# Gate sums per head, and the out-projection's adds at a higher priority, in a hybrid decoder trunk

## The chip, the cores and the metric

The kernel runs on one core of a Trainium2 chip. A core has five engines that run at the same time, each through its own list of instructions in order: TensorE (PE, matmuls), VectorE (DVE), ScalarE (ACT), GpSimd (POOL) and SyncE (SP, which issues DMAs). They wait for each other by semaphores. The metric is the device time of one execution in microseconds, the median of several.

## The reference, cut to what matters

Two residual layers over 512 tokens of width 1024, each followed by a SwiGLU network. The first layer joins a state-space group (16 heads) and a gated linear attention group (GLA, 4 heads), and projects both out. The second is latent attention. The change lies in the first layer, in the GLA group and in the output projection.

```python
def gla_mixer(q, k, v, g, gk_low, gk_w2, gk_b, norm_w):
    gk = jax.nn.log_sigmoid((gk_low @ gk_w2 + gk_b).astype(jnp.float32)) / GLA_GATE_NORM
    gcum = jnp.cumsum(gk.reshape(bsz, nc, Q, H, DK), axis=2)     # within chunks of 64 tokens
    g_last = gcum[:, :, -1]
    q_dec = q * jnp.exp(gcum)
    k_inv = k * jnp.exp(-gcum)
    k_end = k * jnp.exp(g_last[:, :, None] - gcum)
    scores = jnp.where(causal, jnp.einsum('bcihd,bcjhd->bchij', q_dec, k_inv), 0)
    ...
    o = rms_norm(o, norm_w) * jax.nn.silu(g.reshape(bsz, seqlen, H, DV))

def ssd_gla_layer(h, w_in, ..., w_out):
    ...
    return jnp.concatenate([y_ssd, y_gla], axis=-1) @ w_out

x = x + ssd_gla_layer(rms_norm(x, mix_norm_even), ...)
x = x + swiglu(rms_norm(x, ffn_norm[0]), ...)
x = x + mla_layer(rms_norm(x, mix_norm_odd), ...)
x = x + swiglu(rms_norm(x, ffn_norm[1]), ...)
```

## The kernel before

Features lie on the 128 partitions and the 512 tokens along the free dimension. The residual is eight tiles `X[0]` to `X[7]` of 128 x 512 (named x0 to x7), which stay in the on-chip memory. Each product is made of 128 x 512 outputs in one of three PSUM banks (`acc`, line 66), taken in rotation: the next product can only write a bank once the reader of the product three before is done with it.

Every weight arrives by DMA as float32 (`wraw`, two buffers), is split on chip into a rounded part `whi` (ScalarE, line 154) and a rest `wlo` (VectorE, line 155, three buffers each), and each product of a weight block with a split activation is three matmuls (`mm3`, lines 160 to 162). `dense` runs `mm3` over its activation blocks: 24 matmuls for 8 blocks, 12 for 4.

The order on each engine is not written out by hand. A list scheduler orders the instructions by priority, which falls with the place in the program; `tc.high_priority(offset=n)` moves what stands in it ahead by n places. Weights are issued with an offset of 90 (`AHEAD`). Once scheduled, each engine runs its list strictly in order.

The out-projection has four rounds (`out_round`, line 296), each over four of the 16 blocks of 128 mixed features. A round makes eight products of 12 matmuls, numbered 0 to 7 here, two for each weight, and adds product m to `X[m]` (line 304). That add is also what frees the product's `acc` bank. Round 0 runs in the state-space group's last step (line 539), round 1 behind the first GLA head's products (line 706), round 2 and round 3 near the end of the GLA group (lines 717 and 719). In round 3 each finished `X[m]` is also split, squared and summed for the next norm (`Norm.add`).

The GLA group starts with the gates of all heads (lines 571 to 583): a small product per head, ScalarE's Abs, Exp and Ln over the tile `ga` (128 x 2048, four heads side by side), VectorE's minimum into the tile `gm`; then one subtraction over the 2048 columns (line 580) and four running sums, one per head (line 582). `project(h)` makes head h's q and k products and scales them with exponentials of the running sum (tiles e1, e2, e3, el; qd, qp, ki, ke, kp). `inner(h)` makes the scores (lines 644 to 648) in the single bank `a1`, copies them under the mask (lines 651 and 652), transposes kp into the same bank (line 658), and goes on with the state products.

Of the kernel before, what the change touches and what calls it, by code (L numbers as in the profile page):

```python
# [13 lines left out]
ALU = mybir.AluOpType  # L14
# [9 lines left out]
KH = HID // P  # L24
EPS = 1e-6
AHEAD = 90
FIRST = 400
STEPS = 150
VALUES = (2, 3, 7)
# [19 lines left out]
def kernel(ctx: ExitStack, tc: tile.TileContext, A, yT, stop=99):  # L49
    nc = tc.nc  # L50
    V, S, G, E = nc.vector, nc.scalar, nc.gpsimd, nc.tensor
# [9 lines left out]
    def nm(s):  # L61
        cnt[0] += 1
        return f"{s}_{cnt[0]}"

    def acc():
        return pacc.tile([P, T], F32, tag="acc", name=nm("acc"))
# [11 lines left out]
    def aux(tag="st"):  # L78
        while isinstance(phase["tags"][tag], str):
            tag = phase["tags"][tag]  # L80
        return phase["p"].tile([P, T], F32, tag=tag, name=nm(tag), bufs=phase["tags"][tag])
# [4 lines left out]
    X = []  # L86
# [14 lines left out]
    ps = acc()  # L101
# [38 lines left out]
    def weight(src, kc, m):  # L140

        with tc.high_priority(offset=AHEAD):
            return weight_now(src, kc, m)

    def weight_now(src, kc, m):
        raw = wp.tile([P, KD * P], F32, tag="wraw", name=nm("wraw"), bufs=2)
        r = raw[:, :kc * m]
        nc.sync.dma_start(r.rearrange("p (k m) -> p k m", k=kc), src)
        return parts(r, kc, m)
# [14 lines left out]
    def dense(ps, w, xs):  # L164

        n = len(xs)
        for k, (xh, xl) in enumerate(xs):
            last = mm3(ps, w[0][:, k, :], w[1][:, k, :], xh, xl, k == 0, k == n - 1)
        return last
# [40 lines left out]
    def rstd_log(ssq, n, pool, tag):  # L210

        hi = const.tile([P, T], F32R, tag="rsa", name=nm("rsa"))
        lo = const.tile([P, T], F32R, tag="rsb", name=nm("rsb"))
        S.copy(hi, ssq)
        V.tensor_tensor(lo, ssq, hi.bitcast(F32), ALU.subtract)
        ps = aux()
        E.matmul(ps, ones_r, hi, start=True, stop=False)
        E.matmul(ps, ones_r, lo, start=False, stop=True)
        R = pool.tile([P, T], F32, tag=tag, name=nm(tag), bufs=1)
        S.activation(R, ps, AF.Ln, scale=1.0 / n, bias=eps)  # L220
        S.activation(R, R, AF.Exp, scale=-0.5)
        m, t = ssq, const.tile([P, T], F32, tag="rsa", name=nm("rst"))
        V.tensor_scalar(m, ps, 1.0 / n, EPS, ALU.mult, ALU.add)
        V.tensor_tensor(t, R, R, ALU.mult)
        V.scalar_tensor_tensor(t, m, -0.5, t, ALU.mult, ALU.mult)
        V.scalar_tensor_tensor(R, t, 1.5, R, ALU.add, ALU.mult)
        return R
# [61 lines left out]
    with tc.tile_pool(name="sq0", bufs=4) as sq0:  # L289
        for c in range(KD):  # L290
            nrm.square(c, nrm.last, sq0, 4)
        with tc.high_priority(offset=FIRST):
            R = rstd_log(nrm.ssq, D, res, "R")
    xp = nrm.parts

    def out_round(r, parts, nxt=None):

        for m2 in range(4):
            w = weight(A["w_out"][r, m2], 4, 256)
            for j in range(2):  # L300
                m = 2 * m2 + j
                ps = acc()
                dense(ps, (w[0][:, :, j * P:(j + 1) * P], w[1][:, :, j * P:(j + 1) * P]), parts)
                V.tensor_tensor(X[m], X[m], ps, ALU.add)
                if nxt is not None:
                    nxt.add(m)

# [7 lines left out]
    with tc.tile_pool(name="gkp", bufs=1) as gkp:  # L315

        ps = aux("a1")
# [60 lines left out]
        with tc.tile_pool(name="ssd", bufs=2) as sp:  # L378
# [144 lines left out]
            for f in range(8):  # L523
                g = f // 4
                if f % 4 == 0:
                    bc = group(g)
                    if f:
                        bc = spread(*bc)
                    ys, ssq = [], None
                xs = nxt_xs if f == 1 else conv(f, "xs", 3)  # L530
                if f == 0:
                    with tc.high_priority(offset=STEPS):
                        dt, act, acd = steps(mm[0])
                zg = z_gate(f)
                if f == 0:
                    nxt_xs = conv(1, "xs", 3)
                    bc = spread(*bc, mm[1])
                if f == R0F:
                    out_round(0, rounds[0])
                if f == VALUES[0]:  # L540
                    rtok = tok_scalar(R)
                if f in VALUES:
                    values(VALUES.index(f))
                y = core(f, xs, zg, *bc)
                ys.append(y)
                sq = res.tile([P, T], F32, tag="sq", name=nm("ysq"), bufs=2)
                S.activation(sq, y, AF.Square)
                if ssq is not None:
                    V.tensor_tensor(sq, ssq, sq, ALU.add)
                ssq = sq  # L550
                if f % 4 == 3:
                    rounds.append(group_norm(g, ys, ssq))
# [3 lines left out]
        with tc.tile_pool(name="gla", bufs=2) as gp:  # L556
            rmask = gp.tile([P, T], F32, name="rmask", bufs=1)
# [13 lines left out]
            ga = gp.tile([P, 4, T], F32, name="ga", bufs=1)  # L571
            gm = gp.tile([P, 4, T], F32, name="gm", bufs=1)
            for h in range(4):
                ps = aux()
# [2 lines left out]
                V.tensor_scalar(gm[:, h, :], ps, col("gk_b", h), 0.0, ALU.add, ALU.min)  # L577
            S.activation(ga, ga, AF.Exp, scale=-1.0)
            S.activation(ga, ga, AF.Ln, bias=1.0)
            V.tensor_tensor(gm, gm, ga, ALU.subtract)  # L580
            for h in range(4):
                V.tensor_tensor_scan(gm[:, h, :], rmask, gm[:, h, :], 0.0, ALU.mult, ALU.add)
            gcum = gm

            scb = []
# [4 lines left out]
            def project(h):  # L590

                gc = gcum[:, h, :]
                gc8 = gc.rearrange("p (c j) -> p c j", c=8)

                el = gp.tile([P, 8], F32, tag="el", name=nm("el"))
                S.activation(el, gc8[:, :, 63], AF.Exp, scale=1.0 / 16)
                el2 = el.rearrange("p (r two) -> p r two", two=2)

                w = weight(A["w_q"][h], KD, P)
                ps = acc()  # L600
                dense(ps, w, xp)
                e1 = gp.tile([P, T], F32, tag="e1", name=nm("e1"))
                S.activation(e1, gc, AF.Exp, scale=1.0 / 16)
                qd = gp.tile([P, T], F32, tag="qd", name=nm("qd"))
                V.scalar_tensor_tensor(qd, ps, P ** -0.5, R, ALU.mult, ALU.mult)
                V.tensor_tensor(qd, qd, e1, ALU.mult)

                qp = gp.tile([P, 4, 2, 64], F32, tag="qp", name=nm("qp"))
                qd4 = qd.rearrange("p (r two j) -> p r two j", r=4, two=2)
                S.copy(qp[:, :, 0, :], qd4[:, :, 0, :])  # L610
                V.tensor_tensor(qp[:, :, 1, :], qd4[:, :, 1, :],
                                el2[:, :, 0:1].to_broadcast([P, 4, 64]), ALU.mult)

                w = weight(A["w_k"][h], KD, P)
                ps = acc()
                last = dense(ps, w, xp)
                kr = gp.tile([P, T], F32, tag="kr", name=nm("kr"))
                V.tensor_tensor(kr, ps, R, ALU.mult)
                e2 = gp.tile([P, T], F32, tag="e1", name=nm("e1"))
                S.activation(e2, gc, AF.Exp, scale=-1.0 / 16)  # L620
                ki = gp.tile([P, T], F32, tag="ki", name=nm("ki"))
                V.tensor_tensor(ki, kr, e2, ALU.mult)
                e3 = gp.tile([P, T], F32, tag="e1", name=nm("e3"))
                V.tensor_tensor(e3.rearrange("p (c j) -> p c j", c=8),
                                gc8[:, :, 63:64].to_broadcast([P, 8, 64]), gc8, ALU.subtract)
                S.activation(e3, e3, AF.Exp, scale=1.0 / 16)  # L626
                ke = kr
                V.tensor_tensor(ke, kr, e3, ALU.mult)
                kp = gp.tile([P, 4, 2, 64], F32, tag="kp", name=nm("kp"))
                ke4 = ke.rearrange("p (r two j) -> p r two j", r=4, two=2)  # L630
                V.tensor_tensor(kp[:, :, 0, :], ke4[:, :, 0, :],
                                el2[:, :, 1:2].to_broadcast([P, 4, 64]), ALU.mult)
                S.copy(kp[:, :, 1, :], ke4[:, :, 1, :])

                return (qd, qp, ki, ke, kp, el2), last
# [58 lines left out]
            def outer(h, os):  # L694
# [8 lines left out]
                return parts  # L703

            q0, _ = project(0)
            out_round(1, rounds[1])
            q1, last = project(1)
            o0 = inner(0, *q0, last)
            q2, last = project(2)
            o1 = inner(1, *q1, last)  # L710
            p01 = outer(0, o0)
# [58 lines left out]
    with tc.tile_pool(name="mla", bufs=2) as mp, tc.tile_pool(name="mla1", bufs=1) as m1:  # L770
# [30 lines left out]
        ps = acc()  # L801
# [10 lines left out]
        for who, n0, n in (("q", 0, 3), ("kv", 3, 2)):  # L812
            lora[who], ssq = [], None
            for c in range(n):
                w = weight(A["w_dqkv"][n0 + c], KD, P)
                ps = acc()
# [12 lines left out]
            ps = aux()  # L829
# [22 lines left out]
        ps = aux()  # L852
# [14 lines left out]
        ps = aux()  # L867
# [247 lines left out]
```

## Time and profile before

| | us |
|---|---|
| median of 3 runs (1372.68 to 1377.39) | 1374.68 |
| the profiled execution | 1372.01 |
| its span, first to last instruction | 1369.8 |
| PE busy in the span | 1344.3 |
| VectorE busy | 811.9 |
| ScalarE busy | 567.8 |
| mean granted TensorE clock | 0.999 |

A profile is one execution. The span is what its views are measured against; 2.2 us lie around it. In a timeline row stand the start, the time taken, the engine, the line of the kernel, the operation, the tiles (output, arrow, inputs), the shape, and in brackets how long the engine had been idle before and what ended that. Two operations of VectorE overlap by a little, so their starts are closer than their durations.

### The profile page before, as it was taken

To read this page: it belongs to the slowest core of one execution; us is meant where nothing else is said; L and a number is where in the kernel's file an instruction comes from. 1 tells how busy PE (TensorE), PEld (TensorE's weight loads), DVE (VectorE), ACT (ScalarE), POOL (GpSimd) and SP (SyncE) were. 2 spreads that over 40 slices of the span, in tenths; PEclk is the share of its full clock that TensorE was granted. 3 is DMA by queue.
4 is the path that set the end of the run, shared out by engine and by line. 5 is a ranking of instruction groups with operands and counts; after the bars stand their busy time and mean duration, and the time that the engine had idled before them with its cause. 6 is when DMAs were issued, how large, how long until landed. Compare 5 with 4: busy or idle time off the path is not lost.

```text
span 1369.8 us, 16681 instructions
## 1 busy us (share of the span) xinstructions
PE 1344.3 (98%) x6506; PEld 1088.3 (79%) x6506; DVE 811.9 (59%) x1364; ACT 567.8 (41%) x946; POOL 7.8 (1%) x35
## 2 busy tenths in 40 slices
PE   9999999899999999999999999999999999999998
PEld 5798789678888888888888887667588888888887
DVE  7887976778967444444333469776594444443221
ACT  7575623544344322332232348775652322322121
POOL 0000000000000000000000000000000000000000
PEclk9999999999999999999999999999999999999999
DMA  5342232312223233333333321111033333323331
GB/s 177 109 153 79 77 100 73 93 51 89 62 92 106 94 93 105 96 92 95 94 100 100 101 63 59 42 47 62 1 95 105 93 93 101 99 93 108 111 104 63
DMA packets 36781, 122.22 MB, mean 89 GB/s; under 512 B 4768, under 2 KB 5792, under 8 KB 36704
## 3 DMA queue, kind: packets, MB, share of 16 engines
q1 hardware_dynamic: 35888, 120.72, 28.6%
q8 instruction: 51, 0.84, 0.3%
q10 hardware_dynamic: 816, 0.46, 0.1%
q14 instruction: 26, 0.21, 0.1%
HBM read 119.03 MB, written 2.13 MB: 88 GB/s over the span
## 4 chain that ended last, share of the span: by engine, by line
PE 88%; DVE 7%; ACT 3%; issue 1%; DMA 1%; SPq 0%; DVEq 0%; ACTq 0%
PE acc L160 26%; PE acc L161 26%; PE acc L162 26%; PE sco L968 2%; PE ptr L982 1%; PE po L991 1%; DVE wlo L155 1%; PE a L485 1%; PE a L677 1%; DVE cva L397 1%; ACT whi L154 0%; PE a L666 0%; DMA acb<-acd 0%; PE a L471 0%; PE a L679 0%
## 5 line engine op out<-in xcount | busy, mean ns | idle before, releaser
L160 PE MATMUL acc<-xh,whi 128*128 128x512 f32 x1144 | 449.6, 393 | 7.4 <-ACT e L626 4.7
L154 ACT CAST whi<-wraw 128x1024 fp32r<-128x1024 f32 (+2 forms) x221 | 225.8, 1022 | 550.2 <-PE acc L161 449.5
L162 PE MATMUL acc<-xh,wlo 128*128 128x512 f32 x1144 | 448.7, 392 | 0.0
L161 PE MATMUL acc<-xl,whi 128*128 128x512 f32 x1144 | 448.1, 392 | 0.0
L155 DVE TENSOR_TENSOR wlo<-wraw,whi 128x1024 fp32r<-128x1024 f32 (+2 forms) x221 | 261.8, 1185 | 159.3 <-ACT whi L154 159.1
L160 PEld LDWEIGHTS acc<-xh,whi 128*128 128x128 f32 x1144 | 215.2, 188 | 53.2 <-ACT e L626 5.0
L162 PEld LDWEIGHTS acc<-xh,wlo 128*128 128x128 f32 x1144 | 215.1, 188 | 45.1 <-issue 0.7
L161 PEld LDWEIGHTS acc<-xl,whi 128*128 128x128 f32 x1144 | 215.3, 188 | 44.4 <-issue 1.0
L162 PE MATMUL acc<-fhh,wlo 128*128 128x512 f32 x288 | 112.0, 389 | 0.0
L160 PE MATMUL acc<-fhh,whi 128*128 128x512 f32 x288 | 112.0, 389 | 0.0
L161 PE MATMUL acc<-fhl,whi 128*128 128x512 f32 x288 | 112.0, 389 | 0.0
L740 DVE TENSOR_TENSOR fu<-acc,R 128x512 f32<-128x512 f32 x44 | 30.4, 691 | 136.8 <-PE acc L162 136.8
L737 DVE TENSOR_TENSOR fg<-acc,R 128x512 f32<-128x512 f32 x44 | 30.4, 691 | 89.4 <-PE acc L162 89.3
L161 PEld LDWEIGHTS acc<-fhl,whi 128*128 128x128 f32 x288 | 54.1, 188 | 11.3
L162 PEld LDWEIGHTS acc<-fhh,wlo 128*128 128x128 f32 x288 | 54.1, 188 | 11.2
L160 PEld LDWEIGHTS acc<-fhh,whi 128*128 128x128 f32 x288 | 54.1, 188 | 11.1
L161 PE MATMUL acc<-mxl,whi 128*128 128x512 f32 x128 | 50.0, 392 | 0.0
L160 PE MATMUL acc<-mxh,whi 128*128 128x512 f32 x128 | 49.7, 391 | 0.0
L162 PE MATMUL acc<-mxh,wlo 128*128 128x512 f32 x128 | 49.7, 390 | 0.0
L968 PE MATMUL sco<-kT,qT 96*128 96x128 f32 (+3 forms) x128 | 42.8, 445 | 1.5 <-DVE mx L971 1.3
L971 DVE CUSTOM_DVE_ANT_0 sc<-sco,am 128x128 f32<-128x128 f32 (+3 forms) x64 | 30.7, 487 | 13.6 <-PE sco L968 11.5
L973 ACT ACTIVATE sc<-sc,mx 128x128 f32<-128x128 f32 (+3 forms) x64 | 35.7, 561 | 7.3 <-DVE mx L971 7.0
(345 smaller groups left out, 1583.8 us busy)
## 6 DMA issues: line engine op xcount, KB each, us to landing
wraw<-in_w_gate_dram SPq DMA_DIRECT2D x44, 512.0 KB, 3.5
wraw<-in_w_up_dram SPq DMA_DIRECT2D x44, 512.0 KB, 3.5
wraw<-in_w_down_dram SPq DMA_DIRECT2D x32, 512.0 KB, 3.6
wraw<-in_w_out_dram SPq DMA_DIRECT2D x16, 512.0 KB, 3.6
wraw<-in_w_xbc_dram SPq DMA_DIRECT2D x12, 512.0 KB, 3.7
wraw<-in_w_down_dram SPq DMA_DIRECT2D x16, 384.0 KB, 3.1
wraw<-in_w_z_dram SPq DMA_DIRECT2D x8, 512.0 KB, 3.6
wraw<-in_w_v_dram SPq DMA_DIRECT2D x8, 512.0 KB, 3.5
```

The lines of the kernel that those rows point to most:

```text
L154: S.copy(hi[:, :kc * m], r)
L155: V.tensor_tensor(lo[:, :kc * m], r, hi.bitcast(F32)[:, :kc * m], ALU.subtract)
L160: E.matmul(out, ah, bh, start=first, stop=False)
L161: E.matmul(out, ah, bl, start=False, stop=False)
L162: return E.matmul(out, al, bh, start=False, stop=last)
L397: V.scalar_tensor_tensor(a, xpad[:, k:k + T], cw[:, 12 * k + i:12 * k + i + 1], a, ALU.mult, ALU.add)
L485: E.matmul(pd[64 * h:64 * h + 64, c * P:(c + 1) * P], xdt[:, c, h, :], mt[:, h, c, :], start=True, stop=True)
L737: V.tensor_tensor(g, pg, R, ALU.mult)
L740: V.tensor_tensor(u, pu, R, ALU.mult)
L968: E.matmul(ps[:, :n], qts[j][:, b * P:(b + 1) * P], kts[j][:, :n], start=True, stop=True)
L971: V.tensor_tensor_reduce(sc[:, :n], ps[:, :n], am[:, T - n:], -scale, 3e38, ALU.add, ALU.min, mx[:, j:j + 1])
L973: S.activation(sc[:, :n], sc[:, :n], AF.Exp, bias=mx[:, j:j + 1], scale=-1.0, accum_out=sm[:, j:j + 1])
```

## The change

The subtraction over all four heads and the four running sums are taken out of the gates' part. In their place each head's `project(h)` begins with that head's subtraction and running sum. And each add of an out-projection round is issued with a priority offset of 150 places.

```diff
 AHEAD = 90
+FREE = 150
...
                 dense(ps, (w[0][:, :, j * P:(j + 1) * P], w[1][:, :, j * P:(j + 1) * P]), parts)
-                V.tensor_tensor(X[m], X[m], ps, ALU.add)
+                with tc.high_priority(offset=FREE):
+                    V.tensor_tensor(X[m], X[m], ps, ALU.add)
                 if nxt is not None:
...
             S.activation(ga, ga, AF.Ln, bias=1.0)
-            V.tensor_tensor(gm, gm, ga, ALU.subtract)
-            for h in range(4):
-                V.tensor_tensor_scan(gm[:, h, :], rmask, gm[:, h, :], 0.0, ALU.mult, ALU.add)
             gcum = gm
...
                 gc = gcum[:, h, :]
+                V.tensor_tensor(gc, gc, ga[:, h, :], ALU.subtract)
+                V.tensor_tensor_scan(gc, rmask, gc, 0.0, ALU.mult, ALU.add)
                 gc8 = gc.rearrange("p (c j) -> p c j", c=8)
```

The scheduler's lists show what moved. PE's and SP's lists keep their order but for one place (below). The names carry buffer numbers here: x5 is `X[5]`, and most lines of the changed kernel stand one or two further down (the add is L304 before and L306 after; the subtraction moves from L580 to L592, the running sum from L582 to L593).

VectorE from add 4 of round 1 on, before:

```order
L304 TENSOR_TENSOR x4_79<-x4_79,acc_432_2522 128x512
L580 TENSOR_TENSOR gm_2335<-gm_2335,ga_2334 128x2048
L155 TENSOR_TENSOR wlo_449_2628<-wraw_447_2625,whi_448_2627 128x1024
L582 SCALAR_TENSOR_TENSOR gm_2335<-rmask_2320,gm_2335 128x512 x4
L606 TENSOR_TENSOR qd_408_2398<-qd_408_2398,e1_407_2396 128x512
L622 TENSOR_TENSOR ki_416_2439<-kr_414_2435,e1_415_2437 128x512
L611 TENSOR_TENSOR qp_409_2401<-qd_408_2398,el_402_2363 128x4x64
L624 TENSOR_TENSOR e3_417_2441<-gm_2335 128x512
L304 TENSOR_TENSOR x5_81<-x5_81,acc_433_2536 128x512
L304 TENSOR_TENSOR x6_83<-x6_83,acc_437_2556 128x512
L628 TENSOR_TENSOR kr_414_2435<-kr_414_2435,e3_417_2441 128x512
L304 TENSOR_TENSOR x7_85<-x7_85,acc_438_2570 128x512
```

The same place of VectorE's list, now:

```order
L306 TENSOR_TENSOR x4_79<-x4_79,acc_432_2519 128x512
L592 TENSOR_TENSOR gm_2335<-gm_2335,ga_2334 128x512 x2
L306 TENSOR_TENSOR x5_81<-x5_81,acc_433_2533 128x512
L593 SCALAR_TENSOR_TENSOR gm_2335<-rmask_2320,gm_2335 128x512
L156 TENSOR_TENSOR wlo_449_2627<-wraw_447_2624,whi_448_2626 128x1024
L306 TENSOR_TENSOR x6_83<-x6_83,acc_437_2553 128x512
L607 TENSOR_TENSOR qd_408_2395<-qd_408_2395,e1_407_2393 128x512
L623 TENSOR_TENSOR ki_416_2436<-kr_414_2432,e1_415_2434 128x512
L612 TENSOR_TENSOR qp_409_2398<-qd_408_2395,el_402_2360 128x4x64
L625 TENSOR_TENSOR e3_417_2438<-gm_2335 128x512
L306 TENSOR_TENSOR x7_85<-x7_85,acc_438_2567 128x512
L593 SCALAR_TENSOR_TENSOR gm_2335<-rmask_2320,gm_2335 128x512
```

Two subtractions of 512 columns and one running sum now stand where one subtraction of 2048 columns and four running sums stood, and adds 5 and 6 stand ahead of head 0's scalings.

Further on in VectorE's list, at the start of head 1's scalings (qd of buffer 445), before:

```order
L662 TENSOR_TENSOR ed_459_2690<-el_402_2363 128x4
L662 TENSOR_TENSOR ed_495_2854<-el_439_2584 128x4
L605 SCALAR_TENSOR_TENSOR qd_445_2619<-acc_443_2592,R_32_192 128x512
L606 TENSOR_TENSOR qd_445_2619<-qd_445_2619,e1_444_2617 128x512
L155 TENSOR_TENSOR wlo_485_2792<-wraw_483_2789,whi_484_2791 128x1024
```

And now:

```order
L663 TENSOR_TENSOR ed_459_2689<-el_402_2360 128x4
L592 TENSOR_TENSOR gm_2335<-gm_2335,ga_2334 128x512
L663 TENSOR_TENSOR ed_495_2855<-el_439_2583 128x4
L592 TENSOR_TENSOR gm_2335<-gm_2335,ga_2334 128x512
L593 SCALAR_TENSOR_TENSOR gm_2335<-rmask_2320,gm_2335 128x512
L606 SCALAR_TENSOR_TENSOR qd_445_2618<-acc_443_2591,R_32_192 128x512
L593 SCALAR_TENSOR_TENSOR gm_2335<-rmask_2320,gm_2335 128x512
L607 TENSOR_TENSOR qd_445_2618<-qd_445_2618,e1_444_2616 128x512
L156 TENSOR_TENSOR wlo_485_2793<-wraw_483_2790,whi_484_2792 128x1024
```

The subtractions and running sums of heads 2 and 3 have come in between. The scores' copies of head 0 follow some rows later in both.

The one place where PE's list changes is the start of the first SwiGLU network, where the two matmuls of the norm's sum (rsa and rsb) stand among the first product's last matmuls. Before:

```order
L160 MATMUL acc_3853<-xh_3790,whi_3849 128x512
L161 MATMUL acc_3853<-xl_3791,whi_3849 128x512
L162 MATMUL acc_3853<-xh_3790,wlo_3850 128x512
L160 MATMUL acc_3853<-xh_3811,whi_3849 128x512
L161 MATMUL acc_3853<-xl_3812,whi_3849 128x512
L192 MATMUL st_3829<-rsa_3825,ones_r 128x512
```

And now:

```order
L161 MATMUL acc_3856<-xh_3793,whi_3852 128x512
L193 MATMUL st_3832<-rsa_3828,ones_r 128x512
L162 MATMUL acc_3856<-xl_3794,whi_3852 128x512
L163 MATMUL acc_3856<-xh_3793,wlo_3853 128x512
L194 MATMUL st_3832<-rsb_3829,ones_r 128x512
L161 MATMUL acc_3856<-xh_3814,whi_3852 128x512
```

Both matmuls of the sum come four places earlier.

## The prediction

> **What bounds the kernel now.** I read the page first: busy times, then the chain that ended last.
>
> ```profile
> PE 1344.3 (98%) x6506; PEld 1088.3 (79%) x6506; DVE 811.9 (59%) x1364; ACT 567.8 (41%) x946; POOL 7.8 (1%) x35
> ...
> PE 88%; DVE 7%; ACT 3%; issue 1%; DMA 1%; SPq 0%; DVEq 0%; ACTq 0%
> ```
>
> PE (TensorE) is busy for 1344.3 of 1369.8 us, and nothing in the change removes a matmul. So the change can only be worth what it does to PE's idle time, 25.5 us, and to the rate at which PE runs. The view of waits, for PE alone, tells where the largest piece lies; the window around it tells the rate.
>
> ```profile
> PE acc L160 <- ACT e L626: 4.7, 1, 4.7
> PE acc L160 <- ACT qT L951: 3.0, 2, 1.6
> ```
> ```profile
> 262.10 0.39 PE L162 MATMUL acc<-mxh,wlo 128*128 128x512 f32 x1
> 267.15 0.47 PE L160 MATMUL acc<-xh,whi 128*128 128x512 f32 x1 [4.66 <-ACT e L626]
> 267.70 0.63 PE L162 MATMUL acc<-xh,wlo 128*128 128x512 f32 x1
> ...
> 271.34 0.39 PE L162 MATMUL acc<-xh,wlo 128*128 128x512 f32 x1
> ...
> 279.50 0.39 PE L162 MATMUL acc<-xh,wlo 128*128 128x512 f32 x1
> ```
> ```profile
> 267.00:271.00 4.00, 3.85 (x10) 3.14 (x11) 3.42 (x8) 1.23 (x4) 0.00 (x0) 0.58 0.00 0
> ...
> 780.00:1000.00 220.00, 209.26 (x1071) 153.42 (x1070) 161.83 (x456) 144.26 (x326) 1.75 (x3) 1.00 0.16 51
> ```
>
> One wait alone, 4.66 us, is the longest of the whole execution. It falls between out-projection round 1 (its last matmul is at 262.10) and head 1's q product (first matmul at 267.15). Behind it the matmuls take 0.63 us, and in that window the granted clock is 0.58 (the third column from the end); from 271.34 they take 0.39 again.
>
> What ends the wait? The view names the exponential of L626, but this product does not read it. It needs a free bank of `acc` (three banks in rotation), its weights, and xh/xl. VectorE's timeline shows the bank:
>
> ```profile
> 254.37 0.69 DVE L304 TENSOR_TENSOR x<-x,acc 128x512 f32<-128x512 f32 x1
> 256.38 2.29 DVE L580 TENSOR_TENSOR gm<-gm,ga 128x2048 f32<-128x2048 f32 x1 [1.32 <-ACT ga L579]
> 258.59 1.22 DVE L155 TENSOR_TENSOR wlo<-wraw,whi 128x1024 fp32r<-128x1024 f32 x1
> 259.72 4.56 DVE L582 TENSOR_TENSOR_SCAN gm<-rmask,gm 128x512 f32<-128x512 f32 x4
> 264.21 0.66 DVE L606 TENSOR_TENSOR qd<-qd,e 128x512 f32<-128x512 f32 x1
> 264.79 0.68 DVE L622 TENSOR_TENSOR ki<-kr,e 128x512 f32<-128x512 f32 x1
> 265.39 0.41 DVE L611 TENSOR_TENSOR qp<-qd,el 128x256 f32<-128x256 f32 x1
> 265.73 0.68 DVE L624 TENSOR_TENSOR e<-gm 128x512 f32<-128x512 f32 x1
> 266.33 1.27 DVE L304 TENSOR_TENSOR x<-x,acc 128x512 f32<-128x512 f32 x2
> 267.52 0.68 DVE L628 TENSOR_TENSOR kr<-kr,e 128x512 f32<-128x512 f32 x1
> 268.13 0.67 DVE L304 TENSOR_TENSOR x<-x,acc 128x512 f32<-128x512 f32 x1
> ```
>
> Matmuls follow each other by 0.227 us (271.34 to 279.50 holds 36), so a product of 12 takes 2.72. Counting back from 262.10, products 5, 6 and 7 of the round are finished at 257.05, 259.77 and 262.49. Their adds run at 266.33 (two) and 268.13, behind the gates' subtraction, four scans and head 0's scalings. The first add ends at about 267.0, and PE starts at 267.15. The bank is the cause; L626 merely ended at about the same time.
>
> **The change, step by step.** The work in VectorE's queue is a little more than before; its order is what changes. I walk the new order with the durations above: 0.60 us from one 512-wide operation to the next, 0.34 for the 256-wide one, 1.13 for a scan or a weight split (258.59 to 259.72). ScalarE bounds it:
>
> ```profile
> 254.43 1.92 ACT L579 ACTIVATE ga<-ga 128x2048 f32<-128x2048 f32 x1
> 256.86 1.06 ACT L154 CAST whi<-wraw 128x1024 fp32r<-128x1024 f32 x1 [0.52 <-PE acc L161]
> 260.97 0.22 ACT L596 ACTIVATE el<-gm 128x8 f32<-128x8 f32 x1 [1.75 <-DVE gm L582]
> 262.30 1.04 ACT L154 CAST whi<-wraw 128x1024 fp32r<-128x1024 f32 x1
> ```
>
> Subtractions of heads 0 and 1 at 256.38 and 256.98; add 5 at 257.58; scan 0 at 258.18; head 1's k split at 259.31 (its cast ended at 257.92); add 6 at 260.44 (product done 259.77); head 0's qd, ki, qp, e3 at 261.04, 261.64, 262.24, 262.58 (el and the exponentials follow scan 0 from 259.4); add 7 at 263.18. Head 1's q product finds its bank free at 258.3, its k product at 261.1, and the weights of both are split by 260.5. So PE goes on at 262.10 + 0.23 = 262.33 in place of 267.15: **4.82 us**. With the pause goes the slow stretch behind it: 267.15 to 279.50 is 12.35 us for 47 steps, and 47 x 0.2267 is 10.65, so **1.70 us**. Together 6.52.
>
> What is late next? Scans and subtractions of heads 2 and 3 now stand among head 1's scalings, ahead of head 0's masked score copies (L651, L652). These free the one bank `a1`, in which PE's transposes of kp (L658) come next.
>
> ```profile
> 281.26 0.73 DVE L651 COPY_PREDICATED sc<-tri_i,a 64x512 f32<-64x512 int32 x1
> 281.88 0.67 DVE L628 TENSOR_TENSOR kr<-kr,e 128x512 f32<-128x512 f32 x1
> 282.58 0.46 DVE L652 COPY_PREDICATED sc<-tri_i,a 64x256 f32<-64x256 int32 x1
> ```
> ```profile
> 283.30 0.49 PE L658 MATMUL a<-ident,kp 128*128 128x128 f32 x3
> ```
>
> Before, L652 ended at 283.04 and L658 ran at 283.30 with no wait: 0.26 us to spare. Going on: scan 1 at 263.78, head 0's ke 264.91, q split of head 2 at 265.51, kp, ed, two subtractions, then scan 2 at 268.35, head 1's qd 269.48, scan 3 at 270.08, the product with e1 271.2, k split 271.8, qp 272.9, e3 273.3, kr 273.9, ki 274.6, L651 275.2, ke 275.8, L652 at 276.5 until 276.96. PE comes to L658 at 283.30 - 6.52 = 276.78. A wait of about **0.2 us**. Its bounds: nothing, and all four added pieces late, 2 x 0.69 + 2 x 1.2 = 3.8 us. I take 0.2, since the walk uses rows of the same instructions.
>
> A rule speaks against splitting the subtraction. One 2048-wide row takes 2.29 us; the neighbouring 512-wide rows take 0.66 to 0.69. The Trainium skill, "VectorE: DVE Perf Modes", section on the TRN2 errata, says that a fixed latency is paid per instruction, so one large tile pays it once and four pay it four times. This trace agrees in direction: 4 x 0.69 is 2.76 against 2.29. By that rule 0.47 us of queue is added; were all of it on PE's path, the sum below would be 5.8 in place of 6.3. The walk gives the four pieces the time of 512-wide rows, and only two of them stand ahead of an add.
>
> The other rounds. Round 0 and the end of round 3 have these rows:
>
> ```profile
> 185.74 1.23 DVE L155 TENSOR_TENSOR wlo<-wraw,whi 128x1024 fp32r<-128x1024 f32 x1 [0.56 <-ACT whi L154]
> 195.76 0.69 DVE L304 TENSOR_TENSOR x<-x,acc 128x512 f32<-128x512 f32 x1 [2.03 <-PE acc L162]
> ```
> ```profile
> 417.45 0.69 DVE L304 TENSOR_TENSOR x<-x,acc 128x512 f32<-128x512 f32 x1 [0.49 <-PE acc L162]
> ...
> 421.12 0.68 DVE L257 TENSOR_TENSOR sq<-sq,sq 128x512 f32<-128x512 f32 x1
> ```
> ```profile
> 421.84 0.62 ACT L189 CAST rsa<-sq 128x512 fp32r<-128x512 f32 x1 [1.51 <-DVE sq L257]
> ```
> ```profile
> 422.51 0.50 PE L192 MATMUL st<-rsa,ones_r 128*128 128x512 f32 x1
> ```
>
> In round 0 the split of 185.74 comes behind one more add, a convolution tap and a sum, at about 188.2. It is for products 6 and 7, and product 6 starts when product 5 is done, at 195.7: six us of cover. I cost it at nothing; without cover it would be the 2.4 us of its delay. In round 3 the norm's matmul L192 stands four matmuls earlier on PE, 422.51 - 0.9 = 421.6 on the old clock. What it waits for moves too: block 6's split and sum (some 1.25 us) now go ahead of add 7, which runs at about 417.7 in place of 417.45, so the last sum starts at about 420.1 in place of 421.12, and the cast ends near 421.5. That is a tie; I take nothing, between a wait of 0.9 if the sum were no earlier and no gain, since PE did not wait there. SP's weight DMAs keep their order and are issued as splits free the raw buffers; the k split of 258.59 moves to 259.31, 0.7 us later, against a load that is needed two products later.
>
> Sum: 6.52 - 0.2 = **6.3 us**. The profiled execution took 1372.01 us (span 1369.8 and 2.2 around it), so 1365.7 for its like. That execution lies 2.67 below the median shown, 1374.68; the same gain from the median gives **1368.4 us**.
>
> **Rivals.**
> 1. The pause goes, the slow clock was not always there. A pause of 4.66 us need not lower the clock in each execution; one profile shows one. Then the gain is 4.82 - 0.2 = 4.6, and the time 1370.1. For it: from 780 to 1000 PE idles for 10.7 us in pieces of up to 1.6, and the granted clock is 1.00 there, so somewhere between 1.6 and 4.7 us lies what a pause may last. Against it: in this trace it did happen, at 0.58. The Trainium skill, "TensorE: Matmul & The Clock Gate", section "What's actually happening", says that the half rate follows a whole idle window of about 3.4 us which runs freely, so that its phase decides; the trace agrees that a pause of 4.66 us can do it, and no row here shows the phase.
> 2. The stall moves to L658. All of 3.8 us arrives there: 6.5 - 3.8 = 2.7, time 1372.0. For it: the spare time was only 0.26 us, and PE is now 6.5 us earlier. Against: the walk.
> 3. No effect. If L626 were the true releaser, or the adds stayed behind the scans: 1374.7. Against: the order lists add 5 ahead of all scans, and the product does not read L626's tile.
> 4. Slower. VectorE runs in order, so an add put ahead blocks what is behind it until its product ends (the row at 195.76 shows 2.03 us of it). If a weight split stands behind it and the very next product needs that split, PE waits 0.69 + 1.22 = 1.9 us per pair of products. Four rounds have 16 pairs; at half of them 15 us are lost, and the time is 1374.7 - 6.3 + 15 = 1383. It decides from four pairs on. Against it: round 0's split has six us of cover.
>
> **How the numbers follow.** Forecast 60%, rival 1 20%, rival 2 8%, no effect 6%, slower 6%. The three runs of before lie 2.0 below to 2.7 above their median; I give the forecast 1366 to 1371 for that, a us more below, since the profiled execution was already under the lowest run, and reach to rivals 1 and 2 above: 1365 to 1373. That leaves out rivals 3 and 4 and the tails. A measurement of this kernel can tell about 0.3%, 4.1 us, from no change, so faster means below 1370.6. The forecast gives that 92 times in 100, rival 1 60, rival 2 15: 0.55 + 0.12 + 0.01 = 0.68. Slower 0.06 and a tail, 0.07. The rest, 0.25, is within.
>
> **What would show it.** In the changed profile: no PE wait over 0.5 us between the round's last matmul and head 1's q product; every matmul there at 0.39 us; add 5 at about 257.6 ahead of the first scan; head 0's kp transposes with a wait of 0 to 0.5 us on VectorE; the span near 1363.5. I am wrong if a PE wait of several us shows at L658, or at the weights of a round, or if the pause remains under another name.

## The result, and the profile after

| | before | changed |
|---|---|---|
| median of 6 runs, us | 1373.22 | 1365.81 |
| lowest to highest | 1371.39 to 1377.39 | 1365.41 to 1367.81 |
| the profiled execution | 1372.01 | 1365.41 |
| its span | 1369.8 | 1363.2 |

The ratio of the medians is 0.9946, with a 95% interval of 0.993 to 0.9962. The changed kernel is faster by 7.4 us, 0.4 to 0.7%. The forecast was 1368.4 us with a gain of 6.3.

The page of the changed kernel's profile, its span, its busy times and its chain by engine:

```profile
span 1363.2 us, 16686 instructions
...
PE 1342.8 (99%) x6506; PEld 1088.0 (80%) x6506; DVE 812.1 (60%) x1367; ACT 567.9 (42%) x946; POOL 7.8 (1%) x35
...
PE 89%; DVE 7%; ACT 2%; issue 1%; DMA 1%; SPq 0%; DVEq 0%; ACTq 0%
```

The work is the same but for three more instructions on VectorE (1367 for 1364, 0.2 us more). What PE has lost is idle time: 1363.2 - 1342.8 is 20.4 us, for 25.5 before. Its busy time is 1.5 us shorter at the same 6506 matmuls, so some of them run at a higher rate.

Its view of waits for PE (in total, times, longest), over the whole execution first and then for 255 to 300 us alone:

```profile
PE acc L161 <- ACT qT L952: 2.9, 2, 1.6
...
PE a L659 <- DVE sc L653: 0.2, 1, 0.2
```

The longest wait is now one of the attention stage that was there before. Of the wait of 4.7 us nothing is left, and the transposes of kp have a new one of 0.2. PE's timeline around the place (start, time taken) shows both:

```profile
261.41 0.39 PE L163 MATMUL acc<-mxh,wlo 128*128 128x512 f32 x1
261.64 0.39 PE L161 MATMUL acc<-xh,whi 128*128 128x512 f32 x1
...
272.29 0.39 PE L163 MATMUL acc<-xh,wlo 128*128 128x512 f32 x1
276.45 0.52 PE L659 MATMUL a<-ident,kp 128*128 128x128 f32 x3 [0.20 <-DVE sc L653]
```

Head 1's q product starts 0.23 us behind the round's last matmul, one ordinary step, and its matmuls take 0.39 us from the first. From the round's last matmul to the transposes of kp 15.04 us pass, where 21.20 (262.10 to 283.30) passed before: **6.16 us less**. VectorE's timeline of the changed kernel tells why:

```profile
255.75 1.29 DVE L592 TENSOR_TENSOR gm<-gm,ga 128x512 f32<-128x512 f32 x2 [1.38 <-ACT ga L581]
256.96 0.68 DVE L306 TENSOR_TENSOR x<-x,acc 128x512 f32<-128x512 f32 x1
257.56 1.22 DVE L593 TENSOR_TENSOR_SCAN gm<-rmask,gm 128x512 f32<-128x512 f32 x1
258.69 1.20 DVE L156 TENSOR_TENSOR wlo<-wraw,whi 128x1024 fp32r<-128x1024 f32 x1
259.81 0.68 DVE L306 TENSOR_TENSOR x<-x,acc 128x512 f32<-128x512 f32 x1
...
262.55 0.69 DVE L306 TENSOR_TENSOR x<-x,acc 128x512 f32<-128x512 f32 x1
...
275.84 0.46 DVE L653 COPY_PREDICATED sc<-tri_i,a 64x256 f32<-64x256 int32 x1
```

Add 5 has run by 257.64, four microseconds before PE wants its bank. The view of windows, 262 to 300 us (PE's busy time is the second figure, the granted clock the third from the end), of the changed kernel:

```profile
262.00:300.00 38.00, 37.78 (x218) 30.26 (x217) 32.16 (x53) 17.75 (x31) 0.00 (x0) 1.00 0.20 65
```

And the same window of the kernel before:

```profile
262.00:300.00 38.00, 33.33 (x190) 26.51 (x189) 26.11 (x45) 16.04 (x28) 0.00 (x0) 0.96 0.19 61
```

PE is busy 4.45 us more of the same 38, with the clock at 1.00 in place of 0.96, and it runs 218 instructions in place of 190 (the figure behind the x).

### The profile page after: what moved, and what is told of

Its sections match the earlier page's. It is cut to its first block, busy times and chain, and to the rows that moved or that the text cites. A ratio compares the mean times of both kernels' runs of the same rounds, so it can differ in the third digit from the quotient of the medians.

```text
span 1363.2 us, 16686 instructions
## 1 busy us (share of the span) xinstructions
PE 1342.8 (99%) x6506; PEld 1088.0 (80%) x6506; DVE 812.1 (60%) x1367; ACT 567.9 (42%) x946; POOL 7.8 (1%) x35
## 4 chain that ended last, share of the span: by engine, by line
PE 89%; DVE 7%; ACT 2%; issue 1%; DMA 1%; SPq 0%; DVEq 0%; ACTq 0%
PE acc L161 26%; PE acc L162 26%; PE acc L163 26%; PE sco L969 2%; PE ptr L983 1%; PE po L992 1%; DVE wlo L156 1%; PE a L487 1%; PE a L678 1%; PE a L473 0%; DVE cva L399 0%; DMA acb<-acd 0%; PE a L667 0%; PE a L680 0%; PE a L491 0%
```

## The experiments

Each kernel differs from the kernel before, or from the changed one, only by the edit shown. "Local stretch" is the time from the start of round 1's last matmul to the start of the first transpose of kp: 21.20 us before, 15.04 after.

**The gates per head alone.** The kernel before, with the subtraction and running sum in `project(h)`, and the adds at their old priority.

```diff
-            V.tensor_tensor(gm, gm, ga, ALU.subtract)
-            for h in range(4):
-                V.tensor_tensor_scan(gm[:, h, :], rmask, gm[:, h, :], 0.0, ALU.mult, ALU.add)
...
+                V.tensor_tensor(gc, gc, ga[:, h, :], ALU.subtract)
+                V.tensor_tensor_scan(gc, rmask, gc, 0.0, ALU.mult, ALU.add)
```

> Only the gates' part of the change: per-head subtraction and running sum; the adds keep their old priority. Bank theory: VectorE has two subtractions, one scan, a weight split and head 0's scalings ahead of add 5, which then starts near 262.0 us on the clock of before (266.33 before), so PE waits about 0.3 us ahead of head 1's q product, with no slow clock behind it, and again about 0.2 us at the kp transposes: 6.0 us less than before. Rival, that each part brings its own share: about half of the 7.4 us of the whole change, 3 to 4 us less than before, with a pause of 1 us or more left.

Measured: 1368.01 us against 1372.98, ratio 0.9962 (0.9949 to 0.9974), a gain of 5.0. Its timeline:

```profile
263.82 1.28 DVE L305 TENSOR_TENSOR x<-x,acc 128x512 f32<-128x512 f32 x2
264.65 0.47 PE L161 MATMUL acc<-xh,whi 128*128 128x512 f32 x1 [0.49 <-ACT e L626]
```

With three scans out of the way, the add that frees the bank comes at 263.82 and the pause shrinks to 0.49 us. No slow matmul follows. The local stretch is 15.43 us, 0.4 longer than with the whole change. So this half does nearly all of it at this place. The time as a whole is 2.2 us above the changed kernel's. In its profile the round's last matmul is 2.36 us later (263.77 for 261.41), and most of that arises early: PE is busy for 172.69 us of the first 180, for 174.92 in the changed kernel's, and the two kernels have the same code there. A single profile can move by that much on its own account; that the medians differ for this reason is not shown.

**The adds' priority alone.** The kernel before, with the adds at the offset of 150, and the gates together as they were.

```diff
-                V.tensor_tensor(X[m], X[m], ps, ALU.add)
+                with tc.high_priority(offset=FREE):
+                    V.tensor_tensor(X[m], X[m], ps, ALU.add)
```

> Only the adds' higher priority; the subtraction over all heads and the four scans stay together. Bank theory: add 5 follows the 2048-wide subtraction at about 258.6 us on the clock of before, so the pause ahead of head 1's q product is gone with the slow clock; head 1's k split comes behind the scans and head 0's scalings and ends near 268.3, when PE wants it (268.2), so a wait of 0 to 0.3 us there; no wait at the kp transposes: 6.3 us less than before. Rival, that each part brings its own share: 3 to 4 us less than before.

Measured: 1368.46 us, ratio 0.9969 (0.9958 to 0.9981), a gain of 4.5. (The profiled execution took 1371.59 us, the longest of the six; its matmuls run slow for a while at 871 us, of which more below.) The pause ahead of the q product is gone, but a wait of 1.5 us stands at the transposes of kp. The timeline of this kernel, over three engines:

```profile
268.80 1.21 DVE L156 TENSOR_TENSOR wlo<-wraw,whi 128x1024 fp32r<-128x1024 f32 x1
...
274.96 1.05 ACT L155 CAST whi<-wraw 128x1024 fp32r<-128x1024 f32 x1 [1.96 <-DMA wraw<-in_w_k_dram]
...
276.04 1.23 DVE L156 TENSOR_TENSOR wlo<-wraw,whi 128x1024 fp32r<-128x1024 f32 x1 [1.55 <-ACT whi L155]
...
279.83 0.45 DVE L654 COPY_PREDICATED sc<-tri_i,a 64x256 f32<-64x256 int32 x1
...
280.42 0.52 PE L660 MATMUL a<-ident,kp 128*128 128x128 f32 x3 [1.51 <-DVE sc L654]
```

Read it from the top. A weight split stands behind the four scans and the adds and comes only at 268.80, 4.89 us behind the round's last matmul (263.91); in the changed kernel it comes at 258.69, 2.72 ahead of it. It is what frees its raw buffer, so the next load of k weights lands late: ScalarE waits 1.96 us for the DMA, VectorE 1.55 us for ScalarE's cast. VectorE's list is in order, so the masked copy behind that split is late too, and PE waits for it. The expectation had no such wait: it followed the adds and left out the raw buffer's chain. The local stretch is 16.51 us. The two halves don't add up, 5.0 and 4.5 against 7.4 together, because they remove the same wait.

**The priority in round 1 only.** The changed kernel, with the offset taken away from rounds 0, 2 and 3.

```diff
-                with tc.high_priority(offset=FREE):
+                with tc.high_priority(offset=FREE if r == 1 else 0):
```

> The changed kernel with the higher priority in round 1 alone; rounds 0, 2 and 3 keep their old order. If the other rounds are worth nothing, as the prediction has it: the time of the changed kernel within 0.5 us. Rival, that they bring the 1.1 us by which the median gain (7.4) is above the forecast (6.3): 1 us above the changed kernel.

Measured: 1365.97 us, ratio 0.9955 (0.9941 to 0.9969), a local stretch of 15.02 us. The priority in the other three rounds is worth nothing that can be measured.

**A spare bank in place of the change.** The kernel before, in which product 7 of round 1 goes to the eighth PSUM bank, unused in this phase. Nothing on VectorE moves ahead.

```diff
-    open_phase(st=1, a1=1, a2=2)
+    open_phase(st=1, a1=1, a2=2, sp=1)
...
-                ps = acc()
+                ps = aux("sp") if r == 1 and m == 7 else acc()
```

> The kernel of before with its old order; only product 7 of round 1 is written to a spare eighth PSUM bank, so head 1's q product takes the bank of add 4, free since about 255 us. Bank theory: add 5 is still at about 266.3 us, but PE goes on without a pause and at full clock: 6.5 us less than before. Rival, that the exponential of L626 or another input of head 0's scalings releases PE: the pause of 4.7 us stays and the time is that of before.

Measured: 1366.57 us, ratio 0.9955 (0.9942 to 0.9967). Its timeline:

```profile
262.22 0.39 PE L162 MATMUL sp<-mxh,wlo 128*128 128x512 f32 x1
262.44 0.39 PE L160 MATMUL acc<-xh,whi 128*128 128x512 f32 x1
...
266.44 1.28 DVE L304 TENSOR_TENSOR x<-x,acc 128x512 f32<-128x512 f32 x2
...
266.56 0.63 ACT L626 ACTIVATE e<-e 128x512 f32<-128x512 f32 x1 [0.30 <-DVE e L624]
```

Add 5 and the exponential of L626 run as late as before, at 266.44 and 266.56, and PE goes on 0.22 us behind the round's last matmul all the same. So the wait of 4.66 us was for the bank, not for the exponential that the view of waits names. The local stretch is 14.78 us.

**Pauses put back, of four lengths.** The changed kernel, with a reduction on VectorE that reads product 5's bank n times just ahead of add 5. Its result is not used. It keeps the bank busy, and n sets how long: 11, 13, 15 and 17.

```diff
+                    if r == 1 and m == 5:
+                        V.tensor_reduce(junk[:, 0:13], ps.unsqueeze(1).to_broadcast([P, 13, T]), AX.X, ALU.add)
...
     mix = mixp.__enter__()
+    junk = mix.tile([P, 18], F32, name="junk", bufs=1)
```

> The changed kernel with one extra VectorE reduction that reads product 5's bank 11 times over (its result is not used) ahead of add 5 of round 1: add 5 ends near 263.6 us on the changed kernel's clock, so PE pauses about 1.9 us ahead of head 1's q product. Theory, that a short pause does not lower the clock: 0.39 us matmuls behind it. Rival, that each pause does: 0.63 us matmuls.

> The same with 13 readings: a pause of about 2.9 us. Theory (an idle window of about 3.4 us is needed): no slow matmuls. Rival, a limit below 2.9 us: about 8 matmuls of 0.63 us, 1.7 us lost beside the pause.

> The same with 15 readings: a pause of about 4.0 us. Theory of the freely running window of 3.4 us: slow matmuls in less than one execution of two, so the profile more likely shows none; the times spread over two levels 1.7 us apart. Rival, a fixed limit between 1.6 and 4 us of pause: slow matmuls in each execution.

> The same with 17 readings: a pause of about 5.1 us, longer than that of before (4.66). Theory of the freely running window: slow matmuls in about half of the executions. Rival, a fixed limit: in all of them, and 5.1 + 1.7 us above the changed kernel.

| n | median, us (10 runs) | ratio to before | pause, us | slow matmuls last, us | local stretch, us |
|---|---|---|---|---|---|
| 11 | 1370.01 | 0.9974 (0.9963 to 0.9986) | 1.53 | none | 17.55 |
| 13 | 1372.76 | 0.9998 (0.9988 to 1.0009) | 2.59 | 3.3 | 19.83 |
| 15 | 1374.76 | 1.0009 (1.0 to 1.0019) | 3.67 | 5.3 | 22.63 |
| 17 | 1376.16 | 1.002 (1.0011 to 1.003) | 4.72 | 5.3 | 23.69 |

PE's timeline with the pause of n = 13:

```profile
268.56 0.47 PE L161 MATMUL acc<-xh,whi 128*128 128x512 f32 x1 [2.59 <-DVE x L308]
268.87 0.39 PE L162 MATMUL acc<-xl,whi 128*128 128x512 f32 x1
...
269.85 0.63 PE L163 MATMUL acc<-xh,wlo 128*128 128x512 f32 x1
...
272.41 0.63 PE L163 MATMUL acc<-xh,wlo 128*128 128x512 f32 x1
272.84 0.51 PE L161 MATMUL acc<-xh,whi 128*128 128x512 f32 x1
```

And with that of n = 17:

```profile
268.18 0.77 PE L161 MATMUL acc<-xh,whi 128*128 128x512 f32 x1 [4.72 <-DVE x L308]
...
273.01 0.63 PE L163 MATMUL acc<-xh,wlo 128*128 128x512 f32 x1
273.44 0.43 PE L161 MATMUL acc<-xh,whi 128*128 128x512 f32 x1
```

Here the name behind the wait is right: x, the add of L308. With n = 13 the matmuls run at 0.39 us for a microsecond after the pause and only then at 0.63. With n = 17 they are slow from the first. A slow matmul starts 0.43 us behind the one ahead, an ordinary one 0.227. The 12 steps from 268.18 to 273.44 take 5.26 us where 12 x 0.227 is 2.72: the pause of 4.72 costs 2.5 us more behind itself. There were two theories: that a pause must last a whole window of 3.4 us, and that a fixed limit lies between 1.5 and 2.6. The pause of 2.59 speaks against the first. The Trainium skill, "TensorE: Matmul & The Clock Gate", section "What's actually happening", states the first: half rate after at least one idle window of about 3.4 us, which runs freely. The granted clock agrees with such windows in length, and the pause of 2.59 that sufficed does not agree with a whole idle one. The view of windows for n = 13 shows it:

```profile
266.26:269.67 3.41, 1.11 (x5) 0.98 (x6) 3.41 (x4) 1.84 (x2) 0.00 (x0) 1.00 0.00 0
269.67:273.08 3.41, 3.41 (x10) 2.63 (x9) 3.41 (x6) 1.66 (x4) 0.00 (x0) 0.50 0.06 10
273.10:280.00 6.90, 6.90 (x31) 5.68 (x31) 6.12 (x10) 3.65 (x7) 0.00 (x0) 1.00 0.23 74
```

The clock is at 0.50 for one stretch of 3.41 us, and in the 3.41 us ahead of it PE was busy for 1.11. With n = 17 it is at 0.50 from 266.69 to 273.52, twice 3.41.

The local stretches grow by 2.5 to 8.7 us, the medians by 4.2 to 10.35 over the changed kernel's. Between 1.4 and 2.2 us of each median therefore lies outside the stretch, and the medians price more than the pause. Three things in the profiles are not the pause's. In these four kernels the transposes of kp stand three matmuls later in PE's list, which is 0.7 us of each local stretch. The out-projection's matmuls follow each other by 0.233 us (11 steps from 260.50 to 263.06 with n = 17) for 0.227, and with n = 15 and 17 the round's last matmul is about 1 us later than in the changed kernel's second profile (263.14 and 263.06 for 262.06). They do so from round 0 on, at 185 us, long before the reduction runs. The tile for its result stands in the pool from which the mixed features come, but that this makes the steps longer is not shown. And with n = 11, 15 and 17 a slow stretch at 874 us, of the kind described below, costs 1.4 us.

**Both kernels again, for what differs from one execution to the next.** The kernel before twice and the changed kernel once, with no edit.

> The kernel before, unchanged, profiled a second time. Theory: the pause ahead of head 1's q product is in every execution (4.5 to 4.9 us), but the length of the slow stretch behind it depends on the execution: between 1.7 us lost, as in the first profile, and about 2.7, as behind the pauses put into the changed kernel. So here 1.7 to 2.7 us lost between 262 and 280, and the mean granted clock at or under 0.999. Rival: the stretch always loses 1.7, and what executions differ by lies elsewhere, in a second slow stretch near 875 us and in the first 180 us.

> The kernel before, unchanged, a third time. The same two expectations: a slow stretch of another length behind the same pause (1.7 to 2.7 us lost), or always 1.7 and the rest elsewhere.

> The changed kernel, unchanged, profiled a second time. Both theories: no pause over 0.5 us and no slow matmul between 255 and 300 us; 31.28 us PE busy of 31.5 from 262.0 on as before. A slow stretch near 875 us may be there or not; if there is one, the execution takes about 1 to 2 us more than 1365.4.

The changed kernel: 1365.99 us, no pause and no slow matmul there, a local stretch of 14.97 us (262.06 to 277.03), and no wait in the view for 255 to 300 us. The kernel before: 1371.52 and 1374.67. PE's timeline of the first of these two:

```profile
266.06 0.76 PE L160 MATMUL acc<-xh,whi 128*128 128x512 f32 x1 [4.66 <-ACT e L626]
266.62 0.63 PE L161 MATMUL acc<-xl,whi 128*128 128x512 f32 x1
...
278.83 0.39 PE L162 MATMUL acc<-xh,wlo 128*128 128x512 f32 x1
```

From the start of head 1's q product to its k product's last matmul, 47 steps on, 12.77 us pass here, 12.35 in the first profile (267.15 to 279.50) and 12.35 in the third (267.21 to 279.56). At full clock they take 10.65. So the slow stretch cost 1.70 us in the first profile, 2.12 in the second and 1.70 in the third. It was there three times out of three. The granted clock was at 0.50 for 3.41 us in the first (267.67 to 271.08) and in the third, and for 6.83 in the second (263.54 to 270.37), of which 2.5 fell into the pause. The third profile has a second one, far from the change:

```profile
874.36 0.45 PE L160 MATMUL acc<-whi,lh 128*128 128x384 f32 x1 [1.34 <-ACT qT L951]
874.64 0.34 PE L161 MATMUL acc<-wlo,lh 128*128 128x384 f32 x1
...
876.33 0.52 PE L161 MATMUL acc<-wlo,lh 128*128 128x384 f32 x1
...
882.32 0.82 PE L982 MATMUL ptr<-ident,sc 128*128 128x128 f32 x6
```

In the first profile of before the same rows are:

```profile
874.18 0.45 PE L160 MATMUL acc<-whi,lh 128*128 128x384 f32 x1 [1.35 <-ACT qT L951]
874.47 0.33 PE L161 MATMUL acc<-wlo,lh 128*128 128x384 f32 x1
...
879.38 0.85 PE L982 MATMUL ptr<-ident,sc 128*128 128x128 f32 x6
```

The pause is the same, 1.35 and 1.34 us. In the one execution matmuls of 0.34 us follow, in the other some of 0.52, and the way to the transposes of L982 takes 7.96 us in place of 5.20: 2.76 us lost.

Why in the one and not in the other? In each of the 13 profiles all changes of the granted clock lie whole multiples of 3.413 us apart: in the first of before at 267.67, 271.08 and 1370.17, 1 and 322 times. The clock thus keeps to slots of that length, and where they lie against the program differs from one execution to the next. The wait ahead of this matmul, 1.34 or 1.35 us, is in all 13 profiles, between 867 and 878 us. In five of them it begins 1.50 to 2.29 us into a slot, and slow matmuls follow in all five, at a cost of 2.8 us twice and 1.4 three times. In the other eight it begins 1.01 to 1.17 or 2.62 to 3.22 us into one, and none follow. So the same wait costs something or nothing by where it falls in its slot. This was read from the profiles afterwards; no run was made to test it. Both theories were half right: the first stretch's price varies, by 0.4 us, and the larger difference between executions lies elsewhere, at 875 us.

## Why the prediction was right

**What bounds the kernel.** Right. The spare bank shows it by itself: with a free bank the wait is gone, though the add and the exponential come as late as before.

**The pause and the slow stretch, 4.82 + 1.70 us.** Right in mechanism, and in size at the place. The local stretch fell by 6.16 us, and by 6.23 in the second profile of the changed kernel, where 6.3 was forecast.

**The walk through VectorE's list.** Right to within 0.1 us. The round's last matmul is 0.69 us earlier in the changed kernel's profile, so its times are to be read 0.69 later. Add 5 was put at 257.58 and ran at 257.65 (256.96 + 0.69). The masked copy L652 of before was put to end at 276.96 and ended at 276.99 (275.84 + 0.46 + 0.69).

**The new wait, 0.2 us.** The place was the right one. The wait is measured at 0.20, and in the second profile it is too little to show. As time lost it was mis-sized: the transposes start 0.59 us behind the matmul ahead of them (275.86 to 276.45) where 0.24 passed before (283.06 to 283.30), so 0.35 us is lost. The prediction counted from the copy's end and left out the 0.15 us from there to PE's start (276.30 to 276.45). That is why the local stretch fell by 6.16 and not by 6.3. The margin is thin: with the priority alone, the same wait was 1.5 us.

**The other rounds, nothing.** The kernel with the priority in round 1 only gives the same time. So the rival that an add put ahead blocks a weight split has no case in the changed kernel. With the priority alone a weight split did fall back, and cost 1.5 us by another way than the rival's. Nor does the rest of the kernel differ: from the transposes of kp to the end of the span 1086.5 us pass in the first profile of before (283.30 to 1369.8), 1086.7 in the second, and 1086.8 in both of the changed kernel. The four subtractions in place of one took 0.69 us each, as the walk had them; what they added to VectorE's queue cost PE no more than the wait above.

**The tie at the first SwiGLU network, nothing.** Right. In the changed kernel's timeline the norm's matmul (L193) follows its predecessor by 0.22 us:

```profile
414.50 0.39 PE L161 MATMUL acc<-xh,whi 128*128 128x512 f32 x1
414.72 0.50 PE L193 MATMUL st<-rsa,ones_r 128*128 128x512 f32 x1
```

**The rival that the slow clock is not always there.** It fell: three profiles of before out of three have it behind this pause. But the reason given for it, that no pause up to 1.6 us lowers the clock, since it was 1.00 from 780 to 1000 us, was one profile's luck. Behind 1.34 us in that stage the clock did fall, in another execution. That the first profile's stretch behind round 1 was of the shorter kind, 1.70 us and not 2.12, was luck too.

**The time, 1368.4 against 1365.81.** The difference of 2.59 has two parts. The forecast started from the median of three runs, 1374.68; the median of six is 1373.22, which makes 1.46. The gain was 7.4 in place of 6.3, which makes 1.1. The interval of the ratio allows gains of 5.2 to 9.6 us, so 1.1 alone is within what the measurement leaves open. What stands behind it is not settled. Of 31 executions of before that were timed beside the pauses, 16 have a mean granted clock of 0.997 or less and a median of 1374.90; the other 15 have 1372.62. So executions of before that lose more to the clock than the first profile, at 0.999, are common, and the forecast took the loss from that one alone: the term of 1.70 us is one slot of 3.41 us at half the clock, behind one pause. But the mean does not say where the time goes: the second profile of before, at 0.996, took 1371.52, less than the first. Nor is it shown that the change makes the stretch at 874 us rarer. Of the seven profiles without slow matmuls behind round 1 two have it, the priority alone and n = 11; of the six with them, three have it.

## What to carry to other kernels

Look for a bank's reader behind a block of work that nobody is waiting for yet. Here one subtraction and four running sums, three of them for heads whose turn came much later, held up an add that PE needed. Issue such work with the head that uses it, move the add ahead, or give that one product a bank of its own; each alone takes away most or all of the wait, and their gains don't add. The add alone brought a new wait of 1.5 us. When the view names a releaser that the waiting instruction does not read, look at which buffer came free at that time. And price a pause of PE with the slow matmuls behind it, from more than one profile.

## What the runs showed of the hardware

- A pause of 2.59 us was enough for matmuls of 0.63 us in place of 0.39, for 3.3 us and beginning only 1 us after the pause. One of 1.53 us at the same place was not enough. Pauses of 3.67 and 4.72 us brought 5.3 us of them.
- The granted clock keeps to slots of 3.413 us: in all 13 profiles its changes lie whole multiples of that apart, and behind the pauses at this place it was at 0.50 for one slot or two. The slot ahead need not be idle as a whole. At this place one in which PE was busy for 1.27 of 3.40 us was enough (second profile of before, 260.13 to 263.53), one with 1.65 of 3.41 was not (first profile, 260.84 to 264.25).
- That is no limit for every stage. At about 874 us a wait of 1.34 or 1.35 us, in a stage with other waits close by, was followed by slow matmuls in five profiles of 13, those in which it began 1.50 to 2.29 us into a slot, at a cost of 1.4 or 2.8 us. How little work in a slot is too little is not settled.
- In the first 180 us, where all these kernels have the same code, PE was busy for between 172.24 us (the priority alone) and 175.71 (the priority in round 1 only) in single profiles. Profiles that differ by 2 or 3 us in total should be compared by place.
